# Index queries of a two-layer decoder trunk: from token-major columns to a column-major pass of their own

## The chip, the cores and the metric

The kernel runs on one core of a Trainium2 chip, in one launch, from inputs in DRAM to the output in DRAM. The metric is the device time of an execution in microseconds (us); several executions are timed and their median is given. One more execution is profiled: its trace has every instruction of every engine with start and duration, and carries a time of its own. The engines go by the names that the profile gives them: PE (TensorE, matrix products), PEld (its weight loads), DVE (VectorE), ACT (ScalarE), POOL (GpSimd) and SP (SyncE, which here only starts transfers).

## What is computed

Two layers of a decoder trunk on 512 tokens of 1024 channels, all in float32. Each layer projects h = RMSNorm(x) with one wide matrix (8,100 columns, of which 1024 are a gate path and 4096 a merge path), runs four token mixers side by side, gates and merges them, and adds two residuals. The part that the change touches is the indexer of mixer A:

```python
iq = rope(a_iq.reshape(B, S, N_IDX_HEADS, IDX_DIM), positions)     # 4 heads of 32
ik = rope(a_ik[:, :, None, :], positions)[:, :, 0, :]              # one key of 32
idx_logits = jnp.einsum('bqhd,bsd->bqhs', iqb, ik).astype(jnp.float32)
score = jnp.einsum('bqh,bqhs->bqs', iwb.astype(jnp.float32) * IDX_W_SCALE, jax.nn.relu(idx_logits))
score = jnp.where(causal[None], score, neg)
_, sel = lax.top_k(score, topk)                                    # 128 keys of each query
```

The kernel never gathers: it finds the 128 best keys of each query by 16 rounds of "8 largest, then strike them out", and turns what is left into an additive mask for the attention. Queries of the first block of 128 tokens have at most 128 keys, so they need no selection.

## The kernel before

**Products.** Every float32 operand is split into two halves, high = rounded to the fast matrix format and low = value minus high. One float32 product is three matrix products (`mm3`, lines 276 to 281): high x high, high x low, low x high. The high half of a weight chunk is made by ACT (`wh`, line 254), the low half by DVE (`wl`, line 256), from a raw chunk that SP loads (line 226; `split_chunk`). Three raw buffers and six pairs of halves exist.

**Passes.** The program is written as a chain of steps. A step gives PE one pass of products and, around it, lets the other work advance by one stage. There are two kinds of pass over the 8 blocks of 128 input channels:

- `ccol`: 128 columns of the weights on the partitions of the result (column-major), the 512 tokens along the row, 8 x 3 = 24 products of 512 columns into bank `cc`. Most of the input projection is done so, and in the same way the 32 merge passes of a layer (bank `mg`, with 6 products more into `z`).
- `tgroup`: 128 tokens on the partitions (token-major), the weight columns along the row. T1 is such a group, with the values of mixer C (256 columns), the index queries iq (128), the index key ik (32) and the index weights iw (4): 420 columns, 8 x 3 products for each of 4 token blocks, so 96 a layer, into banks `tg`.

**Index queries before.** `use_t1` rotates iq and ik together (160 columns, DVE, lines 722 to 727), makes halves of iq (ACT and DVE, tile `isq`), and after a pass PE turns each head's 128 x 128 block (`iqtr`, line 762, 4 transposes for each of token blocks 1 to 3). ACT copies the result to `iqT`. Its rows hold high, high, low, low of one head, so that one product with the stacked key `ikT` gives the full score (`sc`, line 953).

**What sets the order.** Generators stand in three lists: `front` (what follows the last pass), `back` (stick-breaking, attention and other background) and `idle` (the selection). `yield HOP` hands over to the next generator inside a step, `yield PE` puts what follows behind the step's pass, `yield STEP` ends a generator's share of the step. `later(g, n)` delays g by n steps. `select()` scores a block of queries and then does a number of rounds in each step (`RATES`); it starts `SELECT0` = 8 steps after the passes of mixer A's keys. `mix()` (mixer D's spatial products) starts `MIX0` steps after its inputs. `attend()` needs the masks of query blocks 1 and 3, and the last merge of the layer (n = 0) waits for it (`settle`). The engines execute their own instructions in program order, so what stands first in a queue and waits holds up all behind it.

**The opening** of layer 0 is written out by hand in the string `START`: s, r, h, t, e are stages of the first RMSNorm of a token block (squares, root, scaled h, transposes `htr`, halves hh and hl), Q and P are products of the per-layer embedding p (`ple`, banks later stored to DRAM by E, `ple_out`), w splits the next weight chunk, m*tc* multiplies token block t with chunk c of T1's four chunks (2 blocks of channels each, 6 products), T0 to T2 compute the sines and cosines on DVE and ACT.

**Rotations of mixer A's q and k** (`use_a`) show the other form: DVE multiplies the `cc` bank by tables `sinc` and `cosc` that have the columns on their partitions, four POOL transfers swap the halves of each head (`ay`, line 913), and DVE adds in the next step.

Of the kernel before, what the change touches and what calls it, by code (L numbers as in the profile page):

```python
# [52 lines left out]


TGROUPS = {
    "T1": _span("cv") + _span("iq") + _span("ik") + _span("iw"),
    "T2": _span("av") + _span("dv"),
}
CCOLS = {(n, c): _span(n, P * c, P) for n in ("aq", "ak", "cq", "ck", "bb", "bc", "bx", "du") for c in range(2)}
CCOLS.update({(f"gate{n}", c): _span("gate", W * n + P * c, P) for n in range(4) for c in range(2)})  # L60
MERGES = (1, 3, 2, 0)

# [9 lines left out]
def chunk_plan():  # L72

    plan, step = [], 0
    for l in range(L):
        here = []
        if l == 0:

            here = [("p", 1024, (k, 1), 0, 0) for k in range(L)]

        def tgroup(name, cols, steps):
            nonlocal step
            n = tiles_of(cols)
# [12 lines left out]

        def both(n):
            return [(n, 0), (n, 1)]

        tgroup("T1", 420, 4)  # L100
        ccols(*both("cq"), *both("ck"), *both("aq"), *both("ak"))
        for c in range(2):
            ccols(("bc", c), ("bx", c), ("bb", c))
        ccols(*both("du"))
        tgroup("T2", 512, 4)
        for n in MERGES:
            ccols(*both(f"gate{n}"))
# [17 lines left out]
def lay_weights(w_in, w_branch, w_out, w_ple, w_ple_gate):  # L125
# [6 lines left out]
    for l in range(L):  # L132
        for kind, n, arg, _, _ in PLAN[l]:
# [17 lines left out]

QB, TB, SB, RAWB, WB, LEAD = 10, 25, 24, 3, 6, 4


STICKD, MIX0, SELECT0, ATTEND0, RATES = 3, 2, 8, 5, (1, 2, 3, 2)

START = ("i Q f s0 r0 P00 P01 s1 h0 r1 p1 w P02 P03 E00 t0 h1 e0 E01 P10 s2 r2 t1 E02 P11 E03 w h2 e1 P12 s3 r3 E10 "
         "P13 E11 w t2 E12 h3 m00,10 e2 E13 m01,11 t3 e3 w m20,21 m30,31 T0 T1 w m02,12,22,32 T2 m03,13,23,33")

WARM = 3
HOP, PE, STEP, SUMS, ROOT = "hop", "pe", "step", "sums", "root"
# [18 lines left out]
def hybrid_kernel(ctx: ExitStack, tc: tile.TileContext, w, x, p_t, pos, inv_freq, rows, small, ws_t, b_sp, out):  # L186
# [178 lines left out]
    line = spool.tile([1, D], F32, tag="row", name="line", bufs=1)  # L365
    load(line, bass.AP(tensor=rows.tensor, offset=rows.offset, ap=[[0, 1], [1, D]]))
    fline = load(consts.tile([1, 48], F32, name="fline"), bass.AP(tensor=inv_freq.tensor, offset=inv_freq.offset, ap=[[0, 1], [1, 48]]))
    lift = consts.tile([1, P], F32, name="lift")
    V.memset(lift, 1.0)
    A.preload_act_table_set("silu_and_others")  # L370
    gpre = [bank(f"gpre{k}") for k in range(2)]
    zero = consts.tile([P, 512], BF16, name="zero")
    V.memset(zero, 0.0)
    cold = bank("cold")

# [43 lines left out]
    def make_tables():  # L419
# [30 lines left out]
        for hf in range(2):  # L450
            V.tensor_copy(cos32[:, :, hf], cs[:, :, s])
        yield SUMS
        wide = [T(n, (P, NT, 4, 32)) for n in ("cwide", "swide")]
        for hf in range(4):
            V.tensor_copy(wide[0][:, :, hf], cs[:, :, 0:32])
            if hf % 2:
                V.tensor_scalar(wide[1][:, :, hf], sn[:, :, 0:32], -1.0, None, op0=ALU.mult)
            else:
                V.tensor_copy(wide[1][:, :, hf], sn[:, :, 0:32])
        yield PE  # L460
        turned = [turn_blocks("wtr", w.rearrange("p t a f -> p (t a f)")) for w in wide]
        yield STEP
        for d, ps in zip((cosc, sinc), turned):
            A.copy(d.rearrange("p (b s) -> p b s", b=4), ps)

    def make_masks():
        G.memset(bias0, 0.0)
# [108 lines left out]

    xdram = dram.tile([S, D], F32, name="xdram")

    pdram = dram.tile([L * S, 512], F32, name="pdram")


# [64 lines left out]

    def ple_out(l, t):
        o = T("ple")
        if l or t > 1:
            V.tensor_scalar(o, pps.pop((l, t)), 0.5, None, op0=ALU.mult)  # L650
        else:
            A.mul(o, pps.pop((l, t)), 0.5)
        nc.gpsimd.dma_start(pdram[l * S + t * P:l * S + (t + 1) * P, :], o)

    def some(*tcs):
        for t, c in tcs:
            h, lo = halves[2 + c]
            if t not in banks:
                banks[t] = bank("tg")
            for i in range(2):  # L660
                kt, s = 2 * c + i, slice(420 * i, 420 * i + 420)
                mm3(banks[t][:, :420], hlhs(kt, t), (h[:, s], lo[:, s]), kt == 0, kt == KT - 1)

    gs = [first(t) for t in range(NT)]
    tables = make_tables()
    for o in START.split():
        if o == "i":
            split_first()
        elif o == "Q":
            for t in range(NT):  # L670
                pps[0, t] = bank("ple")
                ple_mm(pps[0, t], pts[0], 0, t, (0,))
        elif o == "f":
            frequencies()
        elif o == "w":
            split_next()
        elif o[0] == "T":
            run_to(tables, SUMS)
        elif o[0] == "p":
            split_p(int(o[1]))  # L680
        elif o[0] == "P":
            l, t = int(o[1]), int(o[2])
            if l:
                pps[l, t] = bank("ple")
            ple_mm(pps[l, t], pts[l], l, t, (0, 1) if l else (1,))
        elif o[0] == "E":
# [9 lines left out]
        split_next()  # L696
    state["step"] = 4
    t1_banks = banks
    back.append(later(tables, 2))

    for l in range(L):
        prm = prms[l]
# [29 lines left out]
        def use_t1(t, ps):  # L732
            half_h(vc[:, t, :, 0], heads(ps[:, 0:256]))
            iw = sm("iw", 4)
            V.tensor_scalar(iw, ps[:, 416:420], IDX_SCALE, None, op0=ALU.mult)
            iws[t] = iw
            r = T("ir")
            rope(r[:, :160], ps[:, 256:416], cos32, sin32, 5, t, "ropei")
            yield HOP
            half_l(vc[:, t, :, 0], vc[:, t, :, 1], heads(ps[:, 0:256]))  # L740

            sk = T("isk")[:, :P].rearrange("p (a b f) -> p a b f", a=2, b=2)
            rk = r[:, 128:160]
            rk2 = rk[:, None, :].to_broadcast([P, 2, 32])
            if t:
                sq = T("isq", (P, 4, 2, 2, 32))
                rq = r[:, :128].rearrange("p (h f) -> p h f", h=4)
                for a in range(2):
                    A.copy(sq[:, :, 0, a].bitcast(F32R), rq)
            for a in range(2):  # L750
                A.copy(sk[:, a, 0].bitcast(F32R), rk)
            yield HOP
            if t:
                for a in range(2):
                    V.tensor_tensor(sq[:, :, 1, a], rq, sq[:, :, 0, a], op=ALU.subtract)
# [3 lines left out]
            if t:  # L759
                tp = bank("iqtr")  # L760
                for h in range(4):
                    nc.tensor.transpose(tp[:, h * P:(h + 1) * P], sq[:, h].rearrange("p a b f -> p (a b f)"), ident)
            tk = bank("iktr")
            nc.tensor.transpose(tk[:, :P], sk.rearrange("p a b f -> p (a b f)"), ident)
            yield STEP
            if t:
                q = T("iqT", dt=F32R)
                A.copy(q, tp)
                iqT[t] = q
            V.tensor_copy(ikT[:, t * P:(t + 1) * P], tk[:, :P])  # L770

        if l:
            tgroup(hlhs, 420, use_t1, 1)
        else:
            for t in range(NT):
                front.append(later(use_t1(t, t1_banks[t]), t // 2))
# [125 lines left out]
        weights_first[0] = False  # L902


        def use_a(ks, c, ps):


# [34 lines left out]
        def select():  # L942

            bias[0] = bias0
            for i in range(1, NT):
                n = (i + 1) * P
                cur = T("cur")
                for h in range(4):
                    if h % 2 == 0:
                        yield PE  # L950
                        ps = [bank("sc") for _ in range(2)]
                        for k in range(2):
                            nc.tensor.matmul(ps[k][:, :n], iqT[i][:, (h + k) * P:(h + k + 1) * P], ikT[:, :n], start=True, stop=True)
                        yield STEP
                    if h == 0:
                        V.tensor_scalar(cur[:, :n], ps[0][:, :n], 0.0, iws[i][:, 0:1], op0=ALU.max, op1=ALU.mult)
# [4 lines left out]
                        V.scalar_tensor_tensor(cur[:, :n], r[:, :n], iws[i][:, h:h + 1], cur[:, :n], op0=ALU.mult, op1=ALU.add)  # L961
                dg = cur[:, i * P:n]
                G.affine_select(out=dg, in_=dg, pattern=[[-1, P]], compare_op=ALU.is_ge, fill=MASKED, base=0, channel_multiplier=1)  # L963
                done = 0
                for _ in range(ROUNDS):
                    if done >= rate["select"]:
# [437 lines left out]
```

## Time and profile before

| | |
|---|---|
| median of 3 runs | 1085.08 us (1084.59 to 1085.77) |
| the profiled execution's own time | 1085.33 us |
| its span in the trace | 1083.6 us |
| PE busy | 1073.3 us, 99% of the span, 5041 matrix instructions |
| PEld busy | 898.2 us, 83% |
| DVE / ACT / POOL busy | 756.4 us (70%) / 476.7 us (44%) / 68.1 us (6%) |
| chain that ended last | PE 82%, DVE 10%, ACT 4%, the rest 4% |

The span is the stretch from the first to the last traced instruction; 1.7 us of the execution's own time lie around it. PE is busy almost without a break, so first PE's own instructions count, and then the few places where it stands still. A caution on "busy": products are pipelined, a product of 512 columns is listed with 390 ns and the next one starts some 227 ns after it. Costs are therefore read from start to start.

### The profile page before, as it was taken

How to read it: one execution, taken by the hardware profiler on the slowest of the kernel's cores; microseconds unless marked ns; L12 is line 12 of the kernel's file. 1: busy time of each engine (PE TensorE's matmuls, PEld its weight loads, DVE VectorE, ACT ScalarE, POOL GpSimd, SP SyncE). 2: the span in 40 equal slices, each digit the busy share in tenths (PEclk: the TensorE clock that was granted, in tenths of full speed). 3: DMA queues.
4: the chain of work that ended last, by engine and by line, in shares of the span. 5: the costliest groups of instructions: out<-in, count | busy, mean ns of one | idle time of the engine just before them, and what ended most of it. 6: DMA issues, size and time to landing. Idle time of an engine off the chain costs nothing.

```text
span 1083.6 us, 13580 instructions
## 1 busy us (share of the span) xinstructions
PE 1073.3 (99%) x5041; PEld 898.2 (83%) x5041; DVE 756.4 (70%) x1401; ACT 476.7 (44%) x821; POOL 68.1 (6%) x127
## 2 busy tenths in 40 slices
PE   8999999999999999999999999999999999999998
PEld 5988888888888888888888888888888888888887
DVE  6869877995988745536685787799779875455472
ACT  6457673433425423434444666444243452333341
POOL 2123001000000000001001220100000000000010
PEclk9999999999999999999999999999999999999999
DMA  7545342322232233362534453222322313325341
GB/s 259 167 132 121 91 139 60 96 98 78 79 97 78 80 109 97 114 224 83 175 121 132 126 127 97 84 61 95 99 95 78 98 61 97 98 97 184 127 136 58
DMA packets 39902, 120.50 MB, mean 111 GB/s; under 512 B 5403, under 2 KB 6171, under 8 KB 39836
## 3 DMA queue, kind: packets, MB, share of 16 engines
q1 hardware_dynamic: 34940, 109.15, 31.6%
q0 software_dynamic: 4896, 10.49, 4.0%
q8 instruction: 39, 0.64, 0.2%
q14 instruction: 27, 0.22, 0.1%
HBM read 107.03 MB, written 6.29 MB: 105 GB/s over the span
## 4 chain that ended last, share of the span: by engine, by line
PE 82%; DVE 10%; ACT 4%; issue 2%; DMA 1%; SPq 0%; POOL 0%; DVEq 0%; ACTq 0%; POOLq 0%
PE mg L281 10%; PE mg L279 10%; PE mg L280 10%; PE tg L280 7%; PE tg L279 7%; PE tg L281 7%; PE cc L279 5%; PE cc L281 5%; PE cc L280 5%; PE z L281 3%; PE z L279 3%; PE z L280 3%; DVE wl L256 2%; DVE csp L861 1%; DMA x<-in_x 1%
## 5 line engine op out<-in xcount | busy, mean ns | idle before, releaser
L256 DVE TENSOR_TENSOR wl<-raw,wh 128x1024 fp32r<-128x1024 f32 (+2 forms) x181 | 217.5, 1206 | 30.3 <-ACT wh L254 29.6
L281 PE MATMUL mg<-hh,wl 128*128 128x512 f32 x512 | 199.5, 390 | 1.3 <-DVE wl L256 1.3
L279 PE MATMUL mg<-hh,wh 128*128 128x512 f32 x512 | 199.7, 390 | 0.0
L280 PE MATMUL mg<-hl,wh 128*128 128x512 f32 x512 | 199.3, 389 | 0.0
L254 ACT CAST wh<-raw 128x1024 fp32r<-128x1024 f32 (+2 forms) x181 | 185.9, 1034 | 11.5 <-DMA raw<-in_w 4.3
L279 PE MATMUL cc<-hh,wh 128*128 128x512 f32 x384 | 150.8, 393 | 0.0
L281 PE MATMUL cc<-hh,wl 128*128 128x512 f32 x384 | 149.6, 390 | 0.0
L280 PE MATMUL cc<-hl,wh 128*128 128x512 f32 x384 | 149.6, 390 | 0.0
L1191 ACT ACTIVATE g<-mg,prm 128x512 f32<-128x512 f32 x64 | 44.2, 690 | 231.4 <-PE mg L281 231.4
L281 PEld LDWEIGHTS mg<-hh,wl 128*128 128x128 f32 x512 | 96.1, 188 | 22.4 <-DVE wl L256 2.2
L280 PEld LDWEIGHTS mg<-hl,wh 128*128 128x128 f32 x512 | 96.1, 188 | 19.9
L279 PEld LDWEIGHTS mg<-hh,wh 128*128 128x128 f32 x512 | 96.1, 188 | 19.7
L1197 DVE SCALAR_TENSOR_TENSOR g<-g,z 128x512 f32<-128x512 f32 x48 | 32.9, 686 | 91.8 <-PE z L281 91.7
L281 PEld LDWEIGHTS cc<-hh,wl 128*128 128x128 f32 x384 | 72.1, 188 | 15.4
L280 PEld LDWEIGHTS cc<-hl,wh 128*128 128x128 f32 x384 | 72.2, 188 | 13.9
L279 PEld LDWEIGHTS cc<-hh,wh 128*128 128x128 f32 x384 | 72.1, 188 | 14.0
L971 DVE MAX8 m<-cur 128x8 f32<-128x256 f32 (+2 forms) x96 | 53.6, 559 | 4.8 <-POOL cur L963 2.8
L972 DVE MATCH_REPLACE8 cur<-m,cur 128x256 f32<-128x256 f32 (+2 forms) x96 | 52.1, 542 | 0.0
L279 PE MATMUL tg<-wh,xh 128*128 128x512 f32 (+1 forms) x136 | 51.8, 381 | 0.0
L281 PE MATMUL tg<-wh,xl 128*128 128x512 f32 (+1 forms) x136 | 51.3, 377 | 0.0
L280 PE MATMUL tg<-wl,xh 128*128 128x512 f32 (+1 forms) x136 | 51.2, 377 | 0.0
L279 PE MATMUL tg<-wh,mh 128*128 128x512 f32 x128 | 50.0, 390 | 0.0
(247 smaller groups left out, 1806.5 us busy)
## 6 DMA issues: line engine op xcount, KB each, us to landing
raw<-in_w SPq DMA_DIRECT2D x171, 512.0 KB, 3.5
raw<-in_w SPq DMA_DIRECT2D x8, 420.0 KB, 3.6
praw<-in_p_t SPq DMA_DIRECT2D x8, 256.0 KB, 5.5
x<-in_x SPq DMA_DIRECT2D x8, 256.0 KB, 5.9
pdram<-ple POOLq DMA_DIRECT2D x8, 256.0 KB, 4.2
ay<-ax POOLq DMA_DIRECT2D x32, 64.0 KB, 1.9
res<-in_x SPq DMA_DIRECT2D x8, 256.0 KB, 6.1
ple<-pdram POOLq DMA_DIRECT2D x8, 256.0 KB, 3.7
```

Source lines behind the costliest of these rows:

```text
L254: A.copy(h[:, c], r[:, c])
L256: V.tensor_tensor(lo[:, c], r[:, c], h[:, c].bitcast(F32), op=ALU.subtract)
L279: nc.tensor.matmul(ps, ah, bh, start=start, stop=False)
L280: nc.tensor.matmul(ps, ah, bl, start=False, stop=False)
L281: nc.tensor.matmul(ps, al, bh, start=False, stop=stop)
L861: V.tensor_tensor_scan(x, a, x, 0.0, op0=ALU.add, op1=ALU.add)
L971: V.max(m8, cur[:, :n])
L972: V.match_replace(cur[:, :n], m8, cur[:, :n], TAKEN)
L1191: A.activation(g, ps, AF.Tanh, bias=b_merge(n, dt), scale=0.5)
L1197: V.scalar_tensor_tensor(g, g, 1.0, z, op0=ALU.add, op1=ALU.mult)
```

## The change

iq leaves T1 (now 292 columns) and becomes a `ccol` pass of its own, after the passes of ck and before those of aq. Its bank has head and dimension on the partitions and the tokens along the row. `use_iq` multiplies it by two new tables, swaps the halves of the heads by 8 POOL transfers of 16 partitions, adds, splits, and stacks high, high, low, low of each head by 16 POOL transfers into four tiles `iqT`, one for a head (before: one for a block of queries). The tables are made at the start by 8 more transposes, written to DRAM, and loaded again in each layer. In the opening, the products of `ple` for layer 1, token blocks 0 and 1, are written as A (the two products with `wh`) and B (that with `wl`), the stages stand in another order, and four of the six evacuations of `ple` that DVE did go to ACT. `mix` starts one step later. In `select`, a step ends between the last score of a block and its first round of top-k. Two constants become pool tiles, and the pool has 26 tiles in place of 25.

```diff
@@ plan of the weight chunks
-    "T1": _span("cv") + _span("iq") + _span("ik") + _span("iw"),
+    "T1": _span("cv") + _span("ik") + _span("iw"),
...
+CCOLS["iq", 0] = _span("iq")
...
-        tgroup("T1", 420, 4)
-        ccols(*both("cq"), *both("ck"), *both("aq"), *both("ak"))
+        tgroup("T1", 292, 4)
+        ccols(*both("cq"), *both("ck"), ("iq", 0), *both("aq"), *both("ak"))
...
-QB, TB, SB, RAWB, WB, LEAD = 10, 25, 24, 3, 6, 4
+QB, TB, SB, RAWB, WB, LEAD = 10, 26, 24, 3, 6, 4
...
-STICKD, MIX0, SELECT0, ATTEND0, RATES = 3, 2, 8, 5, (1, 2, 3, 2)
+STICKD, MIX0, SELECT0, ATTEND0, RATES = 3, 3, 8, 5, (1, 2, 3, 2)
...
-START = ("i Q f s0 r0 P00 P01 s1 h0 r1 p1 w P02 P03 E00 t0 h1 e0 E01 P10 s2 r2 t1 E02 P11 E03 w h2 e1 P12 s3 r3 E10 "
-         "P13 E11 w t2 E12 h3 m00,10 e2 E13 m01,11 t3 e3 w m20,21 m30,31 T0 T1 w m02,12,22,32 T2 m03,13,23,33")
+START = ("i Q f s0 r0 P00 P01 s1 h0 r1 p1 w P02 P03 E00 t0 h1 e0 E01 A10,11 s2 B10,11 t1 E02 r2 E10 w E03 h2 e1 P12 s3 "
+         "E11 P13 m00 r3 w E12 t2 m10 e2 h3 E13 m01,11 t3 e3 w m20,21 m30,31 T0 T1 w m02,12,22,32 T2 m03,13,23,33")
@@ make_tables
-        wide = [T(n, (P, NT, 4, 32)) for n in ("cwide", "swide")]
...
+        for o, n in ((32, 16), (0, 32)):
+            wide = [T(i, (P, NT, P // n, n)) for i in ("cwide", "swide")]
...
+            to = (T("cosi"), T("sini")) if o else (cosc, sinc)
+            for k, (d, ps) in enumerate(zip(to, turned)):
+                A.copy(d.rearrange("p (b s) -> p b s", b=4), ps)
+                if o:
+                    nc.gpsimd.dma_start(itabs[k * P:(k + 1) * P], d)
@@ ple_out
-        if l or t > 1:
+        if l and t < 2:
             V.tensor_scalar(o, pps.pop((l, t)), 0.5, None, op0=ALU.mult)
         else:
             A.mul(o, pps.pop((l, t)), 0.5)
@@ use_t1
-            rope(r[:, :160], ps[:, 256:416], cos32, sin32, 5, t, "ropei")
+            rope(r[:, :32], ps[:, 256:288], cos32, sin32, 1, t, "ropei")
...
-                tp = bank("iqtr")
-                for h in range(4):
-                    nc.tensor.transpose(tp[:, h * P:(h + 1) * P], sq[:, h].rearrange("p a b f -> p (a b f)"), ident)
...
+        itab = [load(T(n), itabs[k * P:(k + 1) * P]) for k, n in enumerate(("cosi", "sini"))]
+
+        def use_iq(ps):
+            (r, x), y = itab, T("iy")
+            V.tensor_tensor(x, ps, x, op=ALU.mult)
+            V.tensor_tensor(r, ps, r, op=ALU.mult)
+            yield HOP
+            for i in range(8):
+                nc.gpsimd.dma_start(y[16 * (i ^ 1):16 * (i ^ 1) + 16, P:], x[16 * i:16 * i + 16, P:])
+            yield STEP
+            V.tensor_tensor(r[:, P:], r[:, P:], y[:, P:], op=ALU.add)
+            yield HOP
+            q = (x.bitcast(F32R), y.bitcast(F32R))
+            yield from split(q[0][:, P:], q[1][:, P:], r[:, P:])
+            yield HOP
+            for h in range(4):
+                iqT[h] = T("iqT", dt=F32R)
+                for a in range(4):
+                    nc.gpsimd.dma_start(iqT[h][32 * a:32 * a + 32, P:], q[a // 2][32 * h:32 * h + 32, P:])
+
+        ccol(use_iq)
@@ select
-                            nc.tensor.matmul(ps[k][:, :n], iqT[i][:, (h + k) * P:(h + k + 1) * P], ikT[:, :n], start=True, stop=True)
+                            nc.tensor.matmul(ps[k][:, :n], iqT[h + k][:, i * P:(i + 1) * P], ikT[:, :n], start=True, stop=True)
...
                 G.affine_select(out=dg, in_=dg, pattern=[[-1, P]], compare_op=ALU.is_ge, fill=MASKED, base=0, channel_multiplier=1)
+                yield STEP
                 done = 0
```

Three places of the order are needed below. The first is DVE's queue in the opening, from the root of token block 3 (`rs`) to the low half of T1's third chunk. Before:

```order
L488 SCALAR_TENSOR_TENSOR rs<-ss 128x1
L650 TENSOR_SCALAR ple<-ple 128x512 x2
L256 TENSOR_TENSOR wl_338<-raw_160,wh_337 128x840
L650 TENSOR_SCALAR ple<-ple 128x512
L596 SCALAR_TENSOR_TENSOR h<-x_113,rs,gpre_84 128x512
L596 SCALAR_TENSOR_TENSOR h<-x_113,rs,gpre_85 128x512
L293 TENSOR_TENSOR hl_143<-htr,hh_142 128x4x128
L293 TENSOR_TENSOR hl_145<-htr,hh_144 128x4x128
L650 TENSOR_SCALAR ple<-ple 128x512
```

and with the change:

```order
L494 SCALAR_TENSOR_TENSOR rs<-ss 128x1
L258 TENSOR_TENSOR wl_346<-raw_161,wh_345 128x584
L295 TENSOR_TENSOR hl_144<-htr,hh_143 128x4x128
L295 TENSOR_TENSOR hl_146<-htr,hh_145 128x4x128
L604 SCALAR_TENSOR_TENSOR h<-x_113,rs,gpre_84 128x512
L604 SCALAR_TENSOR_TENSOR h<-x_113,rs,gpre_85 128x512
```

The evacuations of `ple` are gone from this piece, and the low halves of token block 2 (hl) now stand ahead of the scaled rows h of block 3.

The second is DVE's queue in merge pass 8 of layer 0, where the score of the last block of queries (512 keys) is finished and its top-k begins. The `wl` at the end is the chunk of the next pass. Before:

```order
L961 SCALAR_TENSOR_TENSOR cur<-relu,iw,cur 128x512 x2
L971 MAX m_2660<-cur 128x8
L972 MATCH_REPLACE cur<-m_2660,cur 128x512
L971 MAX m_2663<-cur 128x8
L972 MATCH_REPLACE cur<-m_2663,cur 128x512
L256 TENSOR_TENSOR wl_2697<-raw_2508,wh_2696 128x1024
```

and with the change, in merge passes 11 and 12, where the score of that block now falls:

```order
L990 SCALAR_TENSOR_TENSOR cur<-relu,iw,cur 128x512 x2
L1227 SCALAR_TENSOR_TENSOR g<-g,z 128x512
L1228 TENSOR_TENSOR m_2453<-m_2453,g 128x512
L258 TENSOR_TENSOR wl_2984<-raw_2779,wh_2983 128x1024
L1001 MAX m_2991<-cur 128x8
```

A pass's own work now stands between the score and the first round, and three passes lie between the old place and the new one.

The third is POOL's queue at the passes of mixer A, of which each layer has one. Before:

```order
L793 DMA cql_554<-cql_554 64x512
L913 DMA ay<-ax 32x512 x16
L926 DMA kT<-kT 64x512
L926 DMA kTl<-kTl 64x512
```

and with the change (sini and iy hold the products, then the halves, of the index queries):

```order
L799 DMA cql_555<-cql_555 64x512
L919 DMA iy<-sini 16x384 x8
L942 DMA ay<-ax 32x512 x4
L929 DMA iqT<-sini 32x384 x2
L929 DMA iqT<-iy 32x384 x2
L942 DMA ay<-ax 32x512 x12
L955 DMA kT<-kT 64x512
L955 DMA kTl<-kTl 64x512
```

The pair of `iqT` rows comes four times in a row, once for each head. 24 transfers enter the queue, 16 of them ahead of the `ay` of the second of mixer A's four passes.

## Rows read from the trace of the kernel before

**Rows 1.** The page, busy time of the engines, share of the span, instructions.

```profile
PE 1073.3 (99%) x5041; PEld 898.2 (83%) x5041; DVE 756.4 (70%) x1401; ACT 476.7 (44%) x821; POOL 68.1 (6%) x127
```

**Rows 2.** Waits of PE: line, releaser, us in total, times, longest.

```profile
PE ple L280 <- DVE wl L256: 1.4, 1, 1.4
...
PE mg L281 <- DVE wl L256: 1.3, 2, 0.7
PE mix L279 <- ACT vn L287: 1.1, 2, 0.6
```

**Rows 3.** Timeline of PE, three stretches: start, duration (us), instruction.

```profile
26.38 0.35 PE L280 MATMUL tg<-wl,hh 128*128 128x420 f32 x1
...
30.59 0.35 PE L281 MATMUL tg<-wh,hl 128*128 128x420 f32 x1
...
45.73 0.40 PE L280 MATMUL cc<-hl,wh 128*128 128x512 f32 x1
...
50.73 0.39 PE L281 MATMUL cc<-hh,wl 128*128 128x512 f32 x1
...
1073.57 0.28 PE L280 MATMUL tg<-wl,xh 128*128 128x256 f32 x1
...
1079.09 0.28 PE L281 MATMUL tg<-wh,xl 128*128 128x256 f32 x1
```

**Rows 4.** Groups of PEld: form, count, busy us, mean ns, idle before.

```profile
L279 PEld LDWEIGHTS tg<-wh,xh 128*128 128x128 f32 x136 | 25.6, 188 | 4.5
```

**Rows 5.** Timeline of PE, transposes of one token block's index queries, then the next.

```profile
56.52 0.60 PE L762 MATMUL iqtr<-ident,isq 128*128 128x128 f32 x4
56.95 0.27 PE L764 MATMUL iktr<-ident,isk 128*128 128x128 f32 x1
```

**Rows 6.** Timeline of PE: transposes of token block 3; first product after T1.

```profile
30.78 1.04 PE L496 MATMUL htr<-ident,h 128*128 128x128 f32 x8
...
45.50 0.39 PE L279 MATMUL cc<-hh,wh 128*128 128x512 f32 x1
```

**Rows 7.** Timeline of DVE in the opening.

```profile
25.28 1.28 DVE L650 TENSOR_SCALAR ple<-ple 128x512 f32<-128x512 f32 x2
...
28.02 1.40 DVE L596 SCALAR_TENSOR_TENSOR h<-x,rs,gpre 128x512 f32<-128x512 f32 x2
...
32.03 1.29 DVE L293 TENSOR_TENSOR hl<-htr,hh 128x512 fp32r<-128x512 f32 x2 [0.82 <-ACT hh L287]
33.31 1.05 DVE L256 TENSOR_TENSOR wl<-raw,wh 128x840 fp32r<-128x840 f32 x1
...
39.91 1.03 DVE L256 TENSOR_TENSOR wl<-raw,wh 128x840 fp32r<-128x840 f32 x1 [1.27 <-ACT wh L254]
```

**Rows 8.** Timeline of PE, then DVE, at the start of layer 1's T1.

```profile
558.78 1.03 PE L496 MATMUL htr<-ident,h 128*128 128x128 f32 x8
...
560.31 0.46 PE L280 MATMUL tg<-wl,hh 128*128 128x420 f32 x1 [0.30 <-DVE wl L256]
...
574.02 0.47 PE L279 MATMUL cc<-hh,wh 128*128 128x512 f32 x1
...
557.24 0.88 DVE L1350 TENSOR_SCALAR h<-h,rs 128x512 f32<-128x512 f32 x2 [0.66 <-POOL rs L490]
...
559.24 1.97 DVE L256 TENSOR_TENSOR wl<-raw,wh 128x840 fp32r<-128x840 f32 x2
```

**Rows 9.** Timeline of POOL, then DVE, at mixer A's third pass, layer 0.

```profile
90.87 1.97 POOL L913 DMA_DIRECT2D ay<-ax  x4 [5.36 <-DVE ax L909]
...
95.18 0.68 DVE L915 TENSOR_TENSOR ar<-ar,ay 128x512 f32<-128x512 f32 x1
```

**Rows 10.** The page, transfers: line, queue, count, KB each, median us to landing.

```profile
ay<-ax POOLq DMA_DIRECT2D x32, 64.0 KB, 1.9
```

**Rows 11.** Timeline of DVE in merge pass 8, layer 0.

```profile
275.70 0.69 DVE L971 MAX8 m<-cur 128x8 f32<-128x512 f32 x1 [0.40 <-POOL cur L963]
...
278.62 1.22 DVE L256 TENSOR_TENSOR wl<-raw,wh 128x1024 fp32r<-128x1024 f32 x1
```

More of the change, by code (lines that the diff above doesn't have):

```diff
@@ L367, in hybrid_kernel @@
     fline = load(consts.tile([1, 48], F32, name="fline"), bass.AP(tensor=inv_freq.tensor, offset=inv_freq.offset, ap=[[0, 1], [1, 48]]))
-    lift = consts.tile([1, P], F32, name="lift")
+    lift = T("lift")[:1, :P]
     V.memset(lift, 1.0)
@@ L371, in hybrid_kernel @@
     gpre = [bank(f"gpre{k}") for k in range(2)]
-    zero = consts.tile([P, 512], BF16, name="zero")
+    zero = T("zero", dt=BF16)
     V.memset(zero, 0.0)
@@ L452, in make_tables @@
         yield SUMS
-        wide = [T(n, (P, NT, 4, 32)) for n in ("cwide", "swide")]
[L454 to L464, printed above, removed]
+        for o, n in ((32, 16), (0, 32)):
+            wide = [T(i, (P, NT, P // n, n)) for i in ("cwide", "swide")]
+            for hf in range(0, P // n, 2):
+                s = slice(o, o + n)
+                for w, x in zip(wide, (cs, sn)):
+                    V.tensor_copy(w[:, :, hf], x[:, :, s])
+                V.tensor_copy(wide[0][:, :, hf + 1], cs[:, :, s])
+                V.tensor_scalar(wide[1][:, :, hf + 1], sn[:, :, s], -1.0, None, op0=ALU.mult)
+            yield PE
+            turned = [turn_blocks("wtr", w.rearrange("p t a f -> p (t a f)")) for w in wide]
+            yield STEP
[4 more added lines that the diff above has]
+                    nc.gpsimd.dma_start(itabs[k * P:(k + 1) * P], d)
     def make_masks():
@@ L577, in hybrid_kernel @@
     xdram = dram.tile([S, D], F32, name="xdram")
+    itabs = dram.tile([2 * P, S], F32, name="itabs")
     pdram = dram.tile([L * S, 512], F32, name="pdram")
@@ L660, in some @@
             for i in range(2):
-                kt, s = 2 * c + i, slice(420 * i, 420 * i + 420)
-                mm3(banks[t][:, :420], hlhs(kt, t), (h[:, s], lo[:, s]), kt == 0, kt == KT - 1)
+                kt, s = 2 * c + i, slice(292 * i, 292 * i + 292)
+                mm3(banks[t][:, :292], hlhs(kt, t), (h[:, s], lo[:, s]), kt == 0, kt == KT - 1)
     gs = [first(t) for t in range(NT)]
@@ L685, in hybrid_kernel @@
             ple_mm(pps[l, t], pts[l], l, t, (0, 1) if l else (1,))
+        elif o[0] in "AB":
+            for i in o[1:].split(","):
+                l, t = int(i[0]), int(i[1])
+                h, lo = halves[l]
+                s = slice(t * P, (t + 1) * P)
+                if o[0] == "A":
+                    pps[l, t] = bank("ple")
+                for k in range(2):
+                    cs = slice(512 * k, 512 * k + 512)
+                    if o[0] == "A":
+                        nc.tensor.matmul(pps[l, t], pts[l][k][0][:, s], h[:, cs], start=k == 0, stop=False)
+                        nc.tensor.matmul(pps[l, t], pts[l][k][1][:, s], h[:, cs], start=False, stop=False)
+                    else:
+                        nc.tensor.matmul(pps[l, t], pts[l][k][0][:, s], lo[:, cs], start=False, stop=k == 1)
         elif o[0] == "E":
@@ L698, in hybrid_kernel @@
     t1_banks = banks
-    back.append(later(tables, 2))
+    back.append(tables)
     for l in range(L):
@@ L734, in use_t1 @@
             iw = sm("iw", 4)
-            V.tensor_scalar(iw, ps[:, 416:420], IDX_SCALE, None, op0=ALU.mult)
+            V.tensor_scalar(iw, ps[:, 288:292], IDX_SCALE, None, op0=ALU.mult)
             iws[t] = iw
             r = T("ir")
-            rope(r[:, :160], ps[:, 256:416], cos32, sin32, 5, t, "ropei")
+            rope(r[:, :32], ps[:, 256:288], cos32, sin32, 1, t, "ropei")
             yield HOP
@@ L742, in use_t1 @@
             sk = T("isk")[:, :P].rearrange("p (a b f) -> p a b f", a=2, b=2)
-            rk = r[:, 128:160]
+            rk = r[:, :32]
             rk2 = rk[:, None, :].to_broadcast([P, 2, 32])
[L745 to L749, printed above, removed]
             for a in range(2):
@@ L752, in use_t1 @@
             yield HOP
-            if t:
-                for a in range(2):
-                    V.tensor_tensor(sq[:, :, 1, a], rq, sq[:, :, 0, a], op=ALU.subtract)
             V.tensor_tensor(sk[:, :, 1], rk2, sk[:, :, 0], op=ALU.subtract)
@@ L758, in use_t1 @@
             yield PE
-            if t:
-                tp = bank("iqtr")
-                for h in range(4):
-                    nc.tensor.transpose(tp[:, h * P:(h + 1) * P], sq[:, h].rearrange("p a b f -> p (a b f)"), ident)
             tk = bank("iktr")
@@ L765, in use_t1 @@
             yield STEP
[L766 to L769, printed above, removed]
             V.tensor_copy(ikT[:, t * P:(t + 1) * P], tk[:, :P])
         if l:
-            tgroup(hlhs, 420, use_t1, 1)
+            tgroup(hlhs, 292, use_t1, 1)
         else:
@@ L963, in select @@
                 G.affine_select(out=dg, in_=dg, pattern=[[-1, P]], compare_op=ALU.is_ge, fill=MASKED, base=0, channel_multiplier=1)
+                yield STEP
                 done = 0
```

## The prediction

> **What bounds the kernel now.** First the page's line of busy times: PE is busy for 99% of the span, DVE for 70%, ACT for 44%, POOL for 6% [rows 1]. So the time is what PE's own instructions take plus the few places where PE stands still, and everything else counts only where PE waits for it. Second, PE's list of waits [rows 2]: the ones that the change can reach are 1.4 us for a weight half in the opening, twice 0.65 for weight halves of merge passes, and twice 0.55 for the inputs of mixer D. That is 3.8 us in 1085. Third, the price of a product. Busy time is of no use for it, because products overlap, so I read starts [rows 3]: 22 products of 420 columns from 26.38 to 30.59, 191.4 ns each; 22 of 512 columns in 5.00 us, 227.3 ns; 46 of 256 columns in 5.52 us, 120.0 ns. Between 256 and 420 columns that is 0.435 ns a column, so a product of 292 columns should start every 120.0 + 36 x 0.435 = 135.7 ns. No row has this width; it is an estimate between its two neighbours.
>
> **PE's own work.** T1 has 96 products a layer, which get 191.4 - 135.7 = 55.7 ns cheaper: -5.35 us. The new pass has 24 products of 512 columns, 24 x 0.2273 = +5.45 us. The columns are the same number (96 x 128 = 24 x 512), and so nearly is the time: +0.1 a layer, +0.2 in all. What is won is the turning of the index queries: the four transposes of a token block take 0.43 us, from 56.52 to the next instruction at 56.95 [rows 5], six times in the kernel: -2.6. The tables want 8 more transposes, at the same price +0.86. Sum of PE's work: **-1.5 us**.
>
> How sure is 135.7? Each weight load is listed with 188 ns [rows 4], far more than 135.7, and a change to narrow products leans on that cost. But the products of 256 columns start every 120.0 ns with the same loads, so the loads overlap one another and don't set the pace there. The Trainium skill (Perfetto Trace Analysis, section Identifying the Most-Contended Engine) wants TensorE judged by the busy share of weight loads, not of products; by that share, 83% here, narrowing T1 would win little. The trace speaks against it at 256 columns, and 292 is within 36 of that.
>
> **Waits that go.** (1) The 1.4 us in the opening: PE reaches the product with the low half of the second `ple` matrix before DVE has made it. A (without that half) now stands ahead, other stages lie between, then B. -1.4. (2) `mix` comes a step, some 5.45 us, later; it waited 0.56. -1.1. (3) In merge pass 8 DVE finishes the score and goes straight into top-k at 275.70, and the weights of the next pass stand behind two rounds until 278.62, ready at 279.84 [rows 11]. The extra step puts `wl` ahead of the first round, as the order shows. -1.3. Later passes have rounds before their `wl` too, as now, and show no wait. Sum: **-3.8 us**.
>
> **Waits that come.** T1's products get shorter, but DVE's chain that feeds them does not shrink as much. *Layer 0:* before, `h` of token block 3 starts at 28.02 [rows 7]. Taken from ahead of it are three evacuations of 0.64 and 256 of 840 columns of a `wl` of 1.05 (0.3, and as much of an earlier one); put ahead are the two `hl` of block 2, 1.28. So `h` starts near 28.0 - 1.9 - 0.6 + 1.3 = 26.8. PE now does no 24 products between it and its transposes, which before came at 30.78 [rows 6], 1.36 us after `h`. With the two halves following each other (0.7 for half of `h`, 0.52 for half of the transposes, some 0.65 for ACT's half) the first `hl` of block 3 starts near 28.75; with no overlap near 29.7. Before, from this `hl` (32.03) to the end of T1's last `wl` (40.94) it took 8.9 us, with two `wl` now 0.32 shorter each: 8.25. Then 24 products of 0.136. The first product after T1 would come at 28.75 + 8.25 + 3.26 = 40.3, or 41.2. By PE alone it would be 45.50 - 5.35 - 1.4 = 38.75. The new wait is 1.5 (to 2.4; nothing, if the sine tables' work moves behind it): I take 1.5, since the two halves are separate instructions. *Layer 1:* PE waited 0.30 for `wl` at 560.31 [rows 8]. PE comes to T1's last block some 1.3 us sooner, while `h` on DVE (557.24 after a wait for a root) does not: some 0.25 for `h`, and near 1.1 in place of 0.30 for the third chunk, since `hl` of block 2 and the first of the two `wl` of 559.24 stand ahead. +1.0 (0 to 1.3). Sum: **+2.5 us** (0 to 3.7).
>
> **What costs nothing, and what covers it.** Four evacuations of 0.64 go to ACT, which is busy for 44%; if ACT were late there, the bank would be late for T1, 0.2 to 0.6 once. DVE's rotation and halves on token blocks turn into work of like size on the column-major bank. The constants in the pool only lengthen the pool by one tile. SP loads two more tables a layer, with the weights loaded chunks ahead as cover. Selection and with it the attention end some 4 passes later (the new pass, `yield STEP` for three blocks): the last merge waits for the attention, and before there were 12 passes behind it, now 8. If that cover were gone, PE would wait at the layer's end, a pass (5.45) for each step too many. POOL gets 24 more transfers a layer at 0.49 each [rows 9], 11.8 us. Its queue matters: 16 of them, 7.9 us, now stand ahead of the second `ay` group. POOL idled 5.36 us before such a group, so `ay` would come 7.9 - 5.4 = 2.5 us later, land 1.9 later [rows 10], and DVE's add (95.18 in rows 9) would hold up what is queued behind it, the next `wl` among it, by 2.5 us. PE's cover is that the weights of a pass are made about a pass, 5.45 us, ahead. I put nothing.
>
> **Sum:** -1.5 - 3.8 + 2.5 = -2.8 us, from the profiled execution's own 1085.33 to 1082.5. The median lies 0.25 below that execution, so **1082.3 us**, with the bounds of the terms 1081 to 1083.6. A measurement of this kernel can tell some 0.2%, 2.2 us, from no change; that border (1082.9) runs through this range.
>
> **Rivals.** *The new waits don't show:* DVE gets to T1's last weights early, because the sines and cosines no longer stand ahead. -1.5 - 3.8 = -5.3: 1079.8. For it: DVE has 30% idle. Against it: the 1.27 that DVE itself waited for ACT's `wh` before the last `wl` [rows 7]. Chance 0.12. *The removed waits only move:* with `mix` a step later and top-k a step later, their work meets another pass's `wl`, and the 2.4 of the merge passes and `mix` stay. -1.5 - 1.4 + 2.5 = -0.4: 1084.7. For it: each such wait is a DVE queue that is full for one pass, and the same rounds follow. Against it: of 64 merge passes two showed it. Chance 0.18. *Slower, by POOL's queue:* the 16 transfers start only when `ay` is due, so that POOL's idle time doesn't cover them; DVE then lags by 7.9 us at the add, 2.45 more than a pass, in each layer: +4.9, 1087.2. It decides from a lag above 5.45 on, so from some 0.68 us per transfer if the idle time does cover it. For it: POOL's issues are serial. Against it: POOL is 6% busy. Chance 0.11. *Slower, by the weight loads:* the narrow products start no faster than one load lasts, 188 ns. 192 x (0.188 - 0.1357) = +10.0: 1092.3. The rows of 256 columns speak against it; the gauge named above by the Trainium skill speaks for it. Chance 0.04.
>
> **How the numbers follow.** The forecast has 0.55, of which some 0.37 lie beyond the border and 0.18 within it. Faster: 0.37 + 0.12 = 0.49; within 0.2%: 0.18 + 0.18 = 0.36; slower: 0.11 + 0.04 = 0.15. The range leaves out the slower cases and holds the rest: 1079.3 to 1086.0; the likeliest case's own is 1081 to 1083.6.
>
> **What would show it.** In the profile after: `tg` products about 136 ns from start to start (188 or more would prove the loads rival); no `iqtr`; 16 `wtr` for 8. In PE's waits `ple`, `mg` and `mix` gone from [rows 2] and `tg` there instead with some 2.5 us. The first `cc` product of layer 0 at 40.3, not 45.50, that of layer 1 some 4.4 us earlier than now against the same point. On POOL, `iqT` rows ahead of `ay` with 0.5 us each; on DVE a wait for `ay` at the add, and no `cc` wait of PE behind it. I am wrong if PE shows a wait at the `cc` passes of mixer A or at the last merge, or if waits of other names take the place of those removed.

## The result and the profile after

| | before | after |
|---|---|---|
| median (6 runs each) | 1085.25 us (1084.42 to 1085.77) | 1091.53 us (1090.96 to 1092.84) |
| ratio after to before | | 1.006 (95% interval 1.0047 to 1.0073) |
| the profiled execution, its span | 1085.33, 1083.6 us | 1091.48, 1089.8 us |
| mean granted clock of TensorE | 1.000 | 0.995 |

The change makes the kernel slower by 6.3 us. The forecast said 1082.3, and its range (1079.3 to 1086.0) does not hold the result. The page's line of busy times of the changed kernel, to be set beside [rows 1]:

```profile
PE 1074.1 (99%) x5073; PEld 898.6 (82%) x5073; DVE 755.7 (69%) x1411; ACT 477.6 (44%) x813; POOL 92.2 (8%) x177
```

PE's busy time rose by 0.8 us only, so the busy share tells nothing here. The waits do. PE's list after (line: us in total, times, longest), against [rows 2]:

```profile
PE ctr L832 <- ACT cz L870: 6.6, 2, 3.5
PE tg L282 <- DVE wl L258: 1.4, 2, 1.0
PE cold L380 <- DVE zero L375: 1.4, 1, 1.4
PE tg L281 <- ACT wh L256: 0.8, 1, 0.8
PE htr L502 <- DVE hl L295: 0.2, 1, 0.2
PE htr L502 <- DVE h L1380: 0.2, 1, 0.2
PE ple L704 <- ACT ple L660: 0.2, 1, 0.2
```

All the waits that were to go are gone: `ple` on `wl`, `mg`, `mix`. In their place stands one that the list of before does not have, once a layer: `ctr`, the transposes of mixer C's stick-breaking weights, waits for the exponentials `cz` of ACT. Followed back in layer 0, first POOL's timeline (start, duration, instruction, idle before):

```profile
78.59 1.98 POOL L942 DMA_DIRECT2D ay<-ax  x4 [4.46 <-DVE ax L938]
80.55 1.00 POOL L929 DMA_DIRECT2D iqT<-sini  x2
...
83.45 1.03 POOL L929 DMA_DIRECT2D iqT<-iy  x2
85.58 0.98 POOL L929 DMA_DIRECT2D iqT<-sini  x2 [1.11 <-DMA iqT<-sini]
...
89.42 2.01 POOL L942 DMA_DIRECT2D ay<-ax  x4
```

The inputs of the second `ay` group (`ax`) were ready near 85.2; POOL comes to it at 89.42, behind 16 transfers of `iqT` of 0.5 us each and 1.11 us in which it waited for one of them to land. DVE, ACT and PE behind it:

```profile
89.49 0.43 DVE L868 TENSOR_TENSOR cz<-cz,csp 128x256 f32<-128x256 f32 x1
93.66 0.69 DVE L944 TENSOR_TENSOR ar<-ar,ay 128x512 f32<-128x512 f32 x1 [3.74 <-DMA ay<-ax]
...
114.62 0.43 DVE L868 TENSOR_TENSOR cz<-cz,csp 128x256 f32<-128x256 f32 x1
...
115.08 0.42 ACT L870 ACTIVATE cz<-cz 128x256 f32<-128x256 f32 x1 [1.22 <-DVE cz L868]
...
112.18 0.27 PE L832 MATMUL ctr<-ident,cz 128*128 128x128 f32 x1
115.56 1.50 PE L832 MATMUL ctr<-ident,cz 128*128 128x128 f32 x6 [3.10 <-ACT cz L870]
...
118.35 0.63 PE L282 MATMUL cc<-hl,wh 128*128 128x512 f32 x1
118.78 0.53 PE L283 MATMUL cc<-hh,wl 128*128 128x512 f32 x1
119.15 0.39 PE L281 MATMUL cc<-hh,wh 128*128 128x512 f32 x1
```

DVE stands still for 3.74 us. In the 20 us after that it has 1.8 us of idle time, all of it waiting for ACT, and the stick-breaking chain (DVE and ACT by turns) comes to its last unit late. PE stands still for 3.10 us. Then a second loss: the products after the wait start 0.43 us apart, not 0.227. The stretches of PE's timeline around the two waits (busy us, granted clock, DMA share, GB/s) show why:

```profile
113.00:115.00 2.00, 0.00 (x0) 1.00 0.95 259
115.00:117.00 2.00, 1.45 (x7) 0.66 1.03 256
117.00:119.00 2.00, 2.00 (x8) 0.50 0.02 2
119.00:121.00 2.00, 2.00 (x10) 0.98 0.23 33
...
643.00:645.00 2.00, 0.00 (x0) 0.93 0.77 197
645.00:647.00 2.00, 0.94 (x5) 0.50 1.17 305
647.00:649.00 2.00, 2.00 (x9) 0.50 0.16 23
649.00:651.00 2.00, 2.00 (x6) 0.50 0.17 14
651.00:653.00 2.00, 2.00 (x9) 0.86 0.67 246
```

With the waits of 3.10 us in layer 0 and 3.49 in layer 1 the granted clock falls to 0.50, the lower of its levels (1.2 GHz), and stays there until 119.1 and 651.5.

### The profile page after: what moved, and what is told of

Read it like the earlier page. It is cut to its first block, busy times and chain, and to the rows that moved or that the text cites. A ratio compares the mean times of both kernels' runs of the same rounds, so it can differ in the third digit from the quotient of the medians.

```text
span 1089.8 us, 13775 instructions
## 1 busy us (share of the span) xinstructions
PE 1074.1 (99%) x5073; PEld 898.6 (82%) x5073; DVE 755.7 (69%) x1411; ACT 477.6 (44%) x813; POOL 92.2 (8%) x177
## 4 chain that ended last, share of the span: by engine, by line
PE 87%; DVE 4%; DMA 3%; POOL 2%; ACT 2%; issue 1%; SPq 0%; DVEq 0%; ACTq 0%; POOLq 0%
PE mg L281 11%; PE mg L282 11%; PE mg L283 11%; PE tg L282 7%; PE tg L283 7%; PE tg L281 7%; PE cc L281 6%; PE cc L282 6%; PE cc L283 6%; PE z L281 3%; PE z L283 3%; PE z L282 3%; DMA x<-in_x 1%; DMA ay<-ax 1%; PE ptr L1075 1%
## 5 line engine op out<-in xcount | busy, mean ns | idle before, releaser
L281 PE MATMUL cc<-hh,wh 128*128 128x512 f32 x400 | 158.1, 395 | 0.0
L282 PE MATMUL cc<-hl,wh 128*128 128x512 f32 x400 | 156.6, 392 | 0.0
L283 PE MATMUL cc<-hh,wl 128*128 128x512 f32 x400 | 156.4, 391 | 0.0
L283 PEld LDWEIGHTS cc<-hh,wl 128*128 128x128 f32 x400 | 75.5, 189 | 16.2
L281 PEld LDWEIGHTS cc<-hh,wh 128*128 128x128 f32 x400 | 75.9, 190 | 15.0
L282 PEld LDWEIGHTS cc<-hl,wh 128*128 128x128 f32 x400 | 75.7, 189 | 14.5
```

What stands on the lines that cost most here:

```text
L281: nc.tensor.matmul(ps, ah, bh, start=start, stop=False)
L282: nc.tensor.matmul(ps, ah, bl, start=False, stop=False)
L283: nc.tensor.matmul(ps, al, bh, start=False, stop=stop)
```

## The experiments

The theory (Q in the expectations): POOL's queue makes the second `ay` late, and everything after it follows. The rival (R): the inserted pass moves stick-breaking one pass against mixer A's passes, so that DVE and ACT have too much in one pass, whatever POOL does.

**Fewer transfers ahead of `ay`.** Three kernels differ from the change only in the place of the 16 `iqT` transfers: 8, 12 and none of them ahead of the second `ay` group.

```diff
+# e1_spread, ahead of heads 1, 2 and 3
+                if h:
+                    yield STEP
+# e2_twelve, ahead of head 3
+                if h == 3:
+                    yield STEP
+                    yield HOP
+                    yield HOP
+# e3_behind, ahead of the loop over heads
+            for _ in range(3):
+                yield STEP
+            yield HOP
+            yield HOP
```

> The change with the 16 iqT transfers of a layer spread over three more passes, 4 a pass, so that 8 and not 16 stand between the first and the second group of ay. Nothing else is altered. Theory Q (POOL's queue makes the second ay late, DVE waits for it, PE waits for the stick-breaking exponentials behind, and the clock falls after that wait): 8 transfers of 0.49 are done at about 84.5 us, before ay is wanted at 85.2, so DVE's wait for ay goes, PE's ctr waits of 3.1 and 3.5 us go, the clock stays at 1.00, and the 11 us of waits and halved clock come back: about 1080.5 us. Theory R (the inserted pass moves stick-breaking one pass against mixer A's passes, so that DVE and ACT have too much in one pass, whatever POOL does): the ctr waits stay near 3 us and the time near 1091.

> The change with 12 of the 16 iqT transfers ahead of the second ay group, the last 4 behind it. Theory Q: 12 transfers end at about 86.5 to 87.6 us against the 85.2 at which ay is wanted, so DVE waits 1.0 to 2.1 us, PE's ctr waits are 0.4 to 1.5 us a layer, and with waits that short the clock stays at 1.00: 1081 to 1083.5 us. Were time lost in proportion to the transfers, clock and all, it would be near 1086. Theory R: no difference from the change, 1091.

> The change with all 16 iqT transfers behind the fourth ay group and ahead of mixer A's last key transfers. Theory Q: no wait for ay at all, ctr waits gone, 1080.5 us as with the spread ones; the key transfers kT come up to 8 us later, which nobody waits for until the attention. Theory R: 1091. If the 16 transfers in a row cost time wherever they stand (by the DMA engines, not by POOL's order), the time stays above 1085.

Measured, with before at 1084.97 us on the same chip: 8 ahead 1084.63 us (ratio 0.9995, 0.9986 to 1.0004), 12 ahead 1089.97 (1.0041, 1.0027 to 1.0055), none ahead **1081.30** (0.9965, 0.9952 to 0.9979). With none ahead PE's list has no `ctr` wait, and no new one:

```profile
PE tg L282 <- DVE wl L258: 1.4, 2, 1.0
PE cold L380 <- DVE zero L375: 1.4, 1, 1.4
PE tg L281 <- ACT wh L256: 0.8, 1, 0.8
PE htr L502 <- DVE hl L295: 0.3, 1, 0.3
PE htr L502 <- DVE h L1384: 0.2, 1, 0.2
PE ple L704 <- ACT ple L660: 0.2, 1, 0.2
```

So theory Q holds and R falls: the shifted passes alone cost nothing. But the sizes expected for 8 and 12 were wrong. With 8 ahead, where single executions lie between 1082.33 and 1086.31 us, POOL issues the second `ay` nearly on time, and it still comes late. POOL and DVE of that kernel:

```profile
86.70 1.97 POOL L944 DMA_DIRECT2D ay<-ax  x4 [1.36 <-DVE ar L941]
...
93.27 0.69 DVE L946 TENSOR_TENSOR ar<-ar,ay 128x512 f32<-128x512 f32 x1 [2.48 <-DMA ay<-ax]
```

and from the list of PE's waits:

```profile
PE ctr L832 <- ACT cz L870: 3.2, 2, 1.7
```

The last of the four issues ends at 88.67 and DVE can start at 93.27, 4.6 us later. But the first three of the four transfers land 1.9 to 2.0 us after the start of their issue, as without `iqT` ahead [rows 10]. Only the fourth, issued at 88.18, takes 4.9 us. That is when SyncE starts a weight load (first line; the second is the time from issue to landing of all 32 `ay`, least, median and most):

```profile
88.20 0.33 SPq L228 DMA_DIRECT2D raw<-in_w  x1
...
DMA to landing us min/median/max: 1.8/1.9/4.9
```

The load lands at 92.87 and the fourth transfer at 93.08. With none ahead the same load starts at 88.13, the fourth transfer had been issued at 87.79, and it landed at 89.61. So what `iqT` did here was to push the last issue 0.4 us back, beside a weight load. This is read from the landings; no run moves the load alone. After the waits of 1.7 and 1.5 us of this kernel the clock stays at 1.00.

With 12 ahead POOL issues the second `ay` from 88.88 on. All four then stand behind a load of 88.34 and land at 93.07 to 93.88, and PE waits 2.47 and 2.78 us:

```profile
PE ctr L832 <- ACT cz L870: 5.2, 2, 2.8
```

**The same bytes by another queue.** The transfers of the change at the same place, started by SyncE:

```diff
-                    nc.gpsimd.dma_start(iqT[h][32 * a:32 * a + 32, P:], q[a // 2][32 * h:32 * h + 32, P:])
+                    nc.sync.dma_start(iqT[h][32 * a:32 * a + 32, P:].bitcast(F32), q[a // 2][32 * h:32 * h + 32, P:].bitcast(F32))
```

> The change with the 16 iqT transfers of a layer started by SyncE in place of POOL, at the same place of the program; the same bytes move at the same time. Theory Q1 (POOL's queue is the cause: what stands in it ahead of ay): ay is issued and lands on time, the ctr waits go, 1081.3 us as with the transfers behind (1081 to 1082). Theory Q2 (the DMA engines are the cause: the spread kernel issued its second ay on time at 86.7 and it still landed 4.6 us after its last issue): ay lands late as there, about 1084.6 or more. Should SyncE be held up by these transfers, the weight loads behind them come late and cc products wait for wh or wl.

Measured: **1081.06 us** (1080.66 to 1081.61) against 1085.23, ratio 0.9959 (0.9945 to 0.9973). POOL issues the second `ay` at 86.78, DVE adds at 90.84 without a wait, and `ctr` does not wait:

```profile
86.78 1.96 POOL L942 DMA_DIRECT2D ay<-ax  x4 [5.21 <-ACT wh L256]
...
90.84 0.68 DVE L944 TENSOR_TENSOR ar<-ar,ay 128x512 f32<-128x512 f32 x1
```

So the same 16 transfers, moved in the same stretch, cost nothing once they do not stand in POOL's queue. One more thing differs, though. SyncE is busy with them until 92.2, and the weight load that starts at 88.13 with `iqT` behind starts only at 92.33. No product waits for it, but no load runs beside the second `ay` either. Whether `ay` beside such a load would have landed in time, this run does not show. The Trainium skill (DMA: Bandwidth & Descriptors, section SWDGE vs HWDGE vs iDMA) says that transfers started by GpSimd and those started by SyncE feed different queues inside a DMA engine, which takes turns between them; for `ay` beside `iqT` this run agrees (2.0 to 2.3 us to landing against 1.9). Beside a weight load the traces do not look like turns: in the run with 8 columns below, 1 KB issued 0.16 us after a load lands 3.6 us later, 0.24 behind it. There the measurement decides.

**The suspected cost alone, in the kernel before.** 16 transfers that nobody needs, behind the first `ay` group. Three forms: into one tile (each fourth waits for an earlier one's landing, since they write the same rows), into four tiles, and into four tiles with 8 columns in place of 384. As in the change, the pool has 26 tiles and the two constants are pool tiles in all three (not shown in the diff).

```diff
+            if (ks, c) == (0, 0):
+                ds = [T("dum") for _ in range(4)]
+                for i in range(16):
+                    o = slice(32 * (i % 4), 32 * (i % 4) + 32)
+                    nc.gpsimd.dma_start(ds[i // 4][o, P:], x[o, P:])
```

> The kernel before with 16 more POOL transfers of 32 x 384 a layer, into a tile nobody reads, behind the first ay group of mixer A (and one tile more in the pool for it). They occupy the queue for 8 to 9 us from 78.6, so the second ay moves from 83.6 to about 87. Theory Q: DVE waits some 3 to 4 us for ay; in this kernel the exponentials are ready 1.8 us before PE's ctr, so PE waits 1.3 to 2.2 us a layer and the time is 1087.5 to 1089.5 us, or up to 1094 if the clock falls as well. Theory R: the lag alone does nothing without the shifted passes, about 1085.

> The kernel before with 16 more POOL transfers of 32 x 384 behind the first ay group, into four tiles that nobody reads, so that none of them waits for another one's landing (in the first such run they did, 3.5 and 2.5 us). Theory Q: the second ay is late by 3 to 4.5 us, DVE waits as long, PE waits that less the 1.8 us by which the exponentials are early in this kernel: 1087.5 to 1091 us, up to 1094 if the clock falls after the waits. Theory R (only the shifted passes matter): 1085.

> The same 16 transfers with 32 x 8 elements each, 1 KB in place of 48 KB. The issues stay (16 x 0.49 = 7.9 us on POOL, second ay issued near 86.5 in place of 83.6), the bytes go. If issuing is what makes ay late, DVE's wait is near 2.9 us and the time within 1.5 us of the run with the large ones. If landing behind the bytes is, ay lands 1.9 us after its issue and the time is 2 us or more below the run with the large ones, 1085 to 1087.5.

Measured: one tile 1096.53 us (against 1084.97; DVE waits up to 6.5 us for `ay`; the dummies' waits for one another, which I had not meant, are a part of it); four tiles **1091.64** (against 1085.23, ratio 1.0056); 8 columns 1088.59 (1.0031, 1.0019 to 1.0043). The transfers, put into a kernel without the change, cost 6.4 us; in the change it is 10.2 (1091.53 to 1081.30), where less cover is left and the clock falls for longer. The small ones keep 3.4 of them, which lies between the two expected cases: issues and bytes have about half each. The `ctr` waits of the two last kernels, four tiles first:

```profile
PE ctr L826 <- ACT cz L864: 3.7, 2, 1.9
```

```profile
PE ctr L826 <- ACT cz L864: 1.6, 2, 1.0
```

Both kernels also have about 1 us of waits that the kernel before does not have, 0.8 of it at one `tg` product. Since the pool was changed together with the transfers, these runs do not tell which of the two brought them.

**The other parts of the change, one at a time,** each taken back in the kernel with `iqT` behind (1081.3 us). First the step in `select`:

```diff
-                yield STEP
                 done = 0
```

> The change with iqT behind the ay groups (1081.3 us), less the step that ends between a block's last score and its first top-k round. By the forecast the step removes the waits of merge products for weight halves, 1.3 us in two places: they come back and the time is 1082.3 to 1083. If the later start of selection already moved them away, no difference, 1081.3.

Measured: 1083.41 us (1083.16 to 1084.33), 2.1 above. The `mg` waits are back; the other 0.8 I cannot place.

```profile
PE mg L283 <- DVE wl L258: 1.3, 2, 0.7
```

Then the distance of mixer D:

```diff
-STICKD, MIX0, SELECT0, ATTEND0, RATES = 3, 3, 8, 5, (1, 2, 3, 2)
+STICKD, MIX0, SELECT0, ATTEND0, RATES = 3, 2, 8, 5, (1, 2, 3, 2)
```

> The change with iqT behind the ay groups (1081.3 us) and mixer D started at its old distance, MIX0 = 2. By the forecast the later start removes two waits of PE for mixer D's inputs of 0.55 us each: they come back and the time is 1082.3 to 1082.6. If the shift of the passes by one had already moved mixer D to a place where its inputs are ready, no difference, 1081.3.

Measured: 1081.29 us, no difference, and no `mix` wait in its profile either. The wait goes with the other parts of the change; the later start earns nothing. Then the opening:

```diff
-START = ("i Q f s0 r0 P00 P01 s1 h0 r1 p1 w P02 P03 E00 t0 h1 e0 E01 A10,11 s2 B10,11 t1 E02 r2 E10 w E03 h2 e1 P12 s3 "
-         "E11 P13 m00 r3 w E12 t2 m10 e2 h3 E13 m01,11 t3 e3 w m20,21 m30,31 T0 T1 w m02,12,22,32 T2 m03,13,23,33")
+START = ("i Q f s0 r0 P00 P01 s1 h0 r1 p1 w P02 P03 E00 t0 h1 e0 E01 P10 s2 r2 t1 E02 P11 E03 w h2 e1 P12 s3 r3 E10 "
+         "P13 E11 w t2 E12 h3 m00,10 e2 E13 m01,11 t3 e3 w m20,21 m30,31 T0 T1 w m02,12,22,32 T2 m03,13,23,33")
...
-        if l and t < 2:
+        if l or t > 1:
```

> The change with iqT behind the ay groups (1081.3 us) and the opening of before: its order of stages, its products of ple with the low weight half in place, its evacuations on DVE. By the forecast's sum the new opening saves the wait of 1.4 us for that half and lets the rows h of token block 3 start 1.2 us earlier, with the products of T1 narrower in both: 1082.7 to 1084. If the evacuations on DVE cost more, up to 1085.5. If T1's last chunk sets the end either way (its weight halves wait behind the sines, 1.2 us), only the 1.4 us come back or less: 1081.3 to 1082.7.

Measured: 1083.10 us (1082.43 to 1085.19), 1.8 above; five of the eleven executions, at a lower mean clock (0.997 to 0.998; the others 0.999 to 1.000), are some 2 us slower than the other six. From the first transposes to the first product after T1 it takes 27.44 us (14.08 to 41.52), with the new opening 25.47 (14.95 to 40.42). So the new opening is worth 2.0 us there.

**A version past both.** `iqT` by SyncE and the halves of T1's last weight chunk ahead of the sines:

```diff
-... w m20,21 m30,31 T0 T1 w m02,12,22,32 T2 ...
+... w m20,21 m30,31 w T0 T1 m02,12,22,32 T2 ...
```

> The change with iqT on SyncE's queue (1081.1 us) and, in the opening, the halves of T1's last weight chunk made ahead of the sines and cosines and not between their second and third part. PE waits there 0.84 us for wh and 0.40 us for wl: if these are all that the order costs, the time falls by 1.2 us to 1079.9. If the sines then come too late for the first rotation, or if the raw chunk has not landed, nothing is won: 1081.

Measured: 1080.43 us (1080.29 to 1081.99) against 1085.33, ratio 0.9959 (0.9945 to 0.9972): the best median, 4.9 us below before on the same chip. The waits of 0.84 and 0.40 are gone, and a `ctr` wait of 0.3 has come. The opening is shorter, 23.70 us (15.17 to 38.87) where the SyncE kernel without this edit takes 25.47 (15.08 to 40.55). That the whole time is better than that kernel's is not shown: the two have the same ratio to their own before.

## Why the prediction was wrong

**The terms of the sum held.** PE's own work: T1's products start every 134.0 ns; the estimate was 135.7. From PE's timeline of the changed kernel, 45 starts apart:

```profile
28.52 0.30 PE L283 MATMUL tg<-wh,hl 128*128 128x292 f32 x1
...
34.55 0.29 PE L283 MATMUL tg<-wh,hl 128*128 128x292 f32 x1
```

The weight loads, 188 ns each [rows 4], do not set this pace, so that rival is out. T1 with its new waits: in layer 0 from the first `htr` to the first product after T1 before 30.61 us (14.89 to 45.50), after 25.46 (14.20 to 39.66), -5.15 for a forecast of -5.25; in layer 1 33.38 (540.64 to 574.02) against 29.05 (542.42 to 571.47), -4.33 for -4.35. The waits forecast for T1 are there: 0.84 and 0.40 for the last chunk in layer 0 (the forecast had 1.5; the 0.84 is for ACT's half, where the forecast had followed DVE), 0.23 and 1.01 in layer 1 (0.25 and 1.1). The waits that were to go went, the one of mixer D not by `MIX0` but with the rest. The kernel with `iqT` behind is what the sum was made for: 1081.30 measured, 1082.3 forecast.

**The step that failed is the last one of what was costed at nothing,** POOL's queue: "PE's cover is that the weights of a pass are made about a pass, 5.45 us, ahead. I put nothing." Three things in it were wrong.
- *The wrong consumer.* I took `wl` for the first work that PE would miss. It is `cz`, and its cover is no pass. In the kernel before, ACT ends the last exponential at 116.22 + 0.42 = 116.64 and PE wants it at 118.47, 1.8 us later:

```profile
116.22 0.42 ACT L864 ACTIVATE cz<-cz 128x256 f32<-128x256 f32 x1 [1.99 <-DVE cz L862]
...
118.47 0.27 PE L826 MATMUL ctr<-ident,cz 128*128 128x128 f32 x1
```

  In the changed kernel without the late `ay` (`iqT` behind) ACT ends at 112.61 and PE's first `ctr`, which still has what it needs, is at 112.95: 0.3 us, and a transpose more, are left. That much of R is true: the change used up the cover.

```profile
112.19 0.42 ACT L870 ACTIVATE cz<-cz 128x256 f32<-128x256 f32 x1 [1.22 <-DVE cz L868]
...
112.95 0.27 PE L832 MATMUL ctr<-ident,cz 128*128 128x128 f32 x1
```

- *The lag.* 2.5 us forecast, by issues alone; DVE's wait measured 3.74. Against the run with `iqT` behind, whose first `ay` group comes 0.8 us later, POOL issues the second `ay` 3.9 us late: 7.8 of issues and 1.1 in which it stood for a landing, less 4.97 of idle time ahead of that group. (The 5.36 of the forecast is the idle time ahead of the third.) Then the last transfer takes 2.6 us to land and not 1.8, behind a weight load that lands at 91.56. DVE had 0.8 to spare. Of the lag 3.7 us were left 20 us later: DVE's idle time there is waits for ACT, 1.8 us in both kernels.
- *The clock,* which no term had. Six transposes, the four `cz` products and three `cc` products after the wait take 3.59 us in layer 0 (115.56 to 119.15) and 1.98 (115.92 to 117.90) in the run with 12 ahead, whose clock had not fallen there: 1.6 lost. The same with nine `cc` products in layer 1: 5.90 against 3.33, 2.6 lost.

The account closes. From the `iqT`-behind kernel's span of 1079.5: PE starts its second `ctr` 3.27 us late in layer 0 (115.56 for 112.18 + 0.11) and 3.65 in layer 1 (646.06 for 642.30 + 0.11), the clock takes 1.6 + 2.6, and this execution began its first transposes 0.75 earlier (14.20 for 14.95): 1079.5 + 6.9 + 4.2 - 0.75 = 1089.85, measured 1089.8.

**The rival was there.** "Slower, by POOL's queue" named the place and the mechanism, with a chance of 0.11 and a price of 1087.2. Against it I had put that POOL is 6% busy, which is no argument about a queue at one moment; and its point of decision, a lag above 5.45 us, came from the wrong consumer. With the cover of 1.8 us that the trace of before shows, the lag of 2.5 would already have reached PE.

## What to carry to other kernels

Where work is moved into an in-order queue, follow each instruction behind it to its consumer, and that one's consumer, down to the bottleneck engine, look which loads of other queues start meanwhile, and read the cover from the trace as the time between the end of the last producer and the start of the engine that wants it; the smallest counts, not the one that comes to mind. An engine's busy share says nothing about a burst: 16 transfers at the wrong place cost 10 us, at another place or on another queue none. Before giving up a change that came out slower, see what is new in the waits of the engine that bounds: here the parts that paid are worth 4 us once the burst is moved.

## What the runs showed that I had not expected

- A stretch of 3.10 or 3.49 us without products is followed by 3.6 and 5.5 us at the lower clock, which cost 4.2 us in all. The length of the stretch alone does not tell. With 12 ahead the profiled execution (1087.77 us, mean clock 0.999) kept 2.4 GHz through waits of 2.47 and 2.78 us, and the three others (1089.83 to 1090.55, mean 0.996 to 0.998) were 2 to 3 us slower. With the dummies in four tiles a wait of 1.87 us in layer 1 was followed by 3.4 us at 1.2 GHz.
- POOL does not issue without end while earlier transfers are under way. Where it stood still in the change, it went on once the transfer eight places ahead had landed: in layer 0 at 85.58 for a landing at 85.31, in layer 1 at 613.16 for one at 612.88. What sets the eight is not shown.
- A POOL transfer that is issued beside a weight load of SyncE, or while one is under way, lands behind it, whatever its size. In the change 48 KB issued at 80.55 land at 85.31, behind a load of 80.65 that lands at 85.06; 1 KB issued at 85.81 (8 columns) lands at 89.42, behind a load of 85.65 that lands at 89.18. Of 166 such transfers in eight traces (issued between 0.1 us ahead of a load's start and 1.9 us ahead of its landing) 162 landed after the load and four up to 0.6 us before. With no load under way transfers of the two sizes took 1.8 and 1.5 us.
- 16 transfers of 1 KB still cost 3.4 us, half of what 48 KB each cost.
